# Moving the elementwise work of one streaming-encoder layer from GpSimd to VectorE

## The chip, the core and the metric

The kernel runs on one core of a Trainium2 chip, as one launch. The metric is device microseconds of that core; the median of the three runs of the kernel before is 1533.99 us. PE is TensorE's matrix unit, PEld its weight loads, DVE is VectorE, ACT ScalarE, POOL GpSimd, SP the queue that issues most loads.

## What is computed

One layer over 1024 tokens of width 1024, all in float32. The three branches read one normalised input; their gated sum goes through an output projection, and a SwiGLU feed-forward part follows.

```python
n = rmsnorm(h, norm_mix_pre)
proj = n @ w_in                          # pool input, q, k, v, memory queries, three gates
y_pool = pool_mixer(p_in, w_pool_mix, pool_scale) @ w_pool_o   # trailing means over 2/4/8/16 tokens
y_sb = stick_breaking_attention(q, k, v) @ w_sb_o              # 8 heads, strictly causal
y_x = memory_cross_attention(xq, rmsnorm(mem, norm_mem), w_mem_kv) @ w_x_o
merged = gates[0] * y_pool + gates[1] * y_sb + gates[2] * y_x
h = h + rmsnorm(merged @ w_out, norm_mix_post)
gu = rmsnorm(h, norm_ffn_pre) @ w_ffn_in
ff = (silu(gu[..., :D_FF]) * gu[..., D_FF:]) @ w_ffn_out
h = h + rmsnorm(ff, norm_ffn_post)
```

## The kernel before

Every float32 product is made of three matmuls in a reduced-precision type: each operand is split into a high part (a rounding copy, made by ScalarE) and a low part (operand minus high part, one subtraction of two tiles). `mm3` (L167 to L171) then adds high times high (L169), high times low (L170) and low times high (L171). The low part is the work this document is about. It is made at three places in the code: `split` (L151, subtraction in L164) loads a weight tile and splits it, `parts` (L249 to L251) splits any tile, and `w_parts` calls `parts` for weights. Both take the engine of the subtraction as an argument; most callers leave it at VectorE, and some name `nc.gpsimd`.

The order of the work:

- **Pass over x** (L217 to L235). For each of 8 slices of 128 channels and 2 halves of 512 tokens, ScalarE makes the high part and a square, VectorE the low part (L225), and GpSimd adds the square to the running sum (L233, 14 additions; the first square is written straight into the sum). `pool_step` multiplies.
- **Norms and first operands** (L259 to L306). The memory's sums of squares are added on GpSimd (L294, L297); `rms_rows` makes the row scales, and `inv_root` (L180) takes the power on GpSimd. The operands "11" and "12" of the later products are split, every second one on GpSimd.
- **Operands for Strassen-like products** (L515 to L545). Products by blocks use seven instead of eight multiplications; this needs the operand sums S1 to S4 and "22". Half of S1, all of S4 and all of "22" have their low parts on GpSimd. Three early gate columns (`early`) run in between, with weight low parts on GpSimd.
- **Projections** (`opening`, `pairs`, L436 to L480). Each pair of column blocks takes seven `product` calls. The low parts of the two opening products are GpSimd's, and for the first five pairs also those of S4, S3 and "22". The value projection (L720 to L775) does the same through `two`.
- **Memory attention and pooling** run as background steps between them (`recall`, `pooled`). Of the four pooling groups, the one with window 16 has its product and its sums on GpSimd (`adder`, L649).
- **Stick-breaking attention** (`sticks`, `values`, L835 to L905). ScalarE makes two sigmoids, GpSimd masks them (L856) and sets a start column (L865, L867), VectorE runs a running product (L868) and a multiplication (L874), TensorE transposes (L887) and multiplies with the values (L899, L902). Gate columns fill the gaps (`fill`); each takes a low part on GpSimd (32 in all).
- **Merge and output projection** (L965 to L1060), with weight low parts on GpSimd. These stay.
- **Feed-forward**: eight `opening` calls (L1081), whose 16 weight low parts are on GpSimd, then 11 double blocks and the last product.

Each engine takes its instructions in one fixed order, which the tile framework's scheduler sets when the program is built (from a model of its own), so an instruction that waits holds back all those behind it on the same engine. Loads go through SP's queue, stores through POOL's.

Of the kernel before, what the change touches and what calls it, by code (L numbers as in the profile page):

```python
# [16 lines left out]
KT = D // P  # L17
# [21 lines left out]
def hybrid_block(  # L39
# [177 lines left out]
    for k in range(KT):  # L217
        for c in range(NC):
            xr = t_d()[:, :C]
            load(xr, x[k, c])  # L220
            if c == 0:
                w_units[k] = split(w_pool[k], 3 * P)
            nc.scalar.activation(xgh[k][c], xr, AF.Copy, scale=gain(G_PRE, k))
            xgl[k][c] = (t_b1 if k < 4 else t_b2)(F32R)
            nc.vector.scalar_tensor_tensor(  # L225
                xgl[k][c], xr, gain(G_PRE, k), xgh[k][c].bitcast(F32), ALU.mult, ALU.subtract
            )
            if k == 0:
                nc.scalar.activation(ssum[c], xr, AF.Square)
            else:  # L230
                sq = t_c()[:, :C]
                nc.scalar.activation(sq, xr, AF.Square)
                nc.gpsimd.tensor_add(ssum[c], ssum[c], sq)  # L233
        if k > 3:
            pool_step(k - 4)  # L235
# [43 lines left out]
    for c in range(NC):  # L279
# [24 lines left out]
    for q in range(HK):  # L304
        u = normed_x(q + HK, 0, t_d()[:, :C])
        A["12"][q] = parts(u, t_act(), t_act(), nc.vector if q % 2 else nc.gpsimd)  # L306
# [129 lines left out]
    def opening(raw, sink):  # L436
        (b11, b12), (b21, b22) = raw
        X, Y = ps_a(), ps_a()
        product(X, w_parts(b11, nc.gpsimd), "11", True)
        p1 = copied(X)  # L440
        product(Y, w_parts(b21, nc.gpsimd), "12", True)
# [4 lines left out]
    def pairs(jobs, raws=None, pool=("S4", "S3", "22")):  # L446
# [3 lines left out]

        def some(u, a):
            return w_parts(u, nc.gpsimd if a in pool else nc.vector)

        opened = [opening(raws[j], jobs[j][1]) for j in range(ahead)]
        for j, (_, sink) in enumerate(jobs):
# [6 lines left out]
            product(Y, some(t, "S1"), "S1", True)  # L462
# [3 lines left out]
            product(X, some(t, "S2"), "S2")  # L466
            s2 = copied(X)
            product(Y, some(b22, "S4"), "S4")
# [4 lines left out]
            product(X, some(b12, "S3"), "S3")  # L473
# [5 lines left out]
            product(X, some(b21, "22"), "22")  # L479
# [42 lines left out]
    for q in range(HK):  # L522
# [3 lines left out]
        A["S1"][q] = parts(sums[q], t_act(), t_act(), nc.vector if q % 2 else nc.gpsimd)  # L526
# [7 lines left out]
    for q in range(HK):  # L534
# [3 lines left out]
        A["S4"][q] = parts(u, t_a(F32R), t_a(F32R), nc.gpsimd)  # L538
# [3 lines left out]
    for q in range(HK):  # L542
        A["22"][q] = parts(a22[q], t_act(), t_act(), nc.gpsimd)
# [107 lines left out]
    def pooled(g, c):  # L651
        def step():
            win = 2 << g
            adder = nc.vector if g < 3 else nc.gpsimd
# [7 lines left out]
            adder.tensor_mul(p_in[:, :C], p_in[:, :C], rbc[c])  # L662
            s = p_in
            step_, width = 1, C + 16
            while step_ < win:
                width -= step_
                nxt = t_c()
                adder.tensor_add(nxt[:, :width], s[:, :width], s[:, step_ : step_ + width])
# [63 lines left out]
    def two(us, lo=nc.gpsimd):  # L732
        return [w_parts(u, lo) for u in us]
# [22 lines left out]
    v_product(Y, two(b11, nc.vector), "S1", True)  # L756
# [3 lines left out]
    v_product(X, two(b11, nc.vector), "S2")  # L760
# [40 lines left out]
    pairs([(lambda m=m: quarters(w_gate, m), to_gate(0, m)) for m in range(0, KT, 2)], pool=())  # L801
# [293 lines left out]
    opened = [opening(j, j < HOLD, nc.gpsimd) for j in range(LEAD)]  # L1095
# [297 lines left out]
```

## Time and profile before

| what | us |
|---|---|
| median of 3 runs (lowest, highest) | 1533.99 (1530.56, 1535.62) |
| the profiled execution | 1532.7 |
| its span | 1531.0 |
| PE, DVE, ACT, POOL busy in the span | 1453.5, 1042.6, 705.2, 530.2 |
| mean granted clock of TensorE | 0.984 |

The profile shows one execution. Busy time is the time in which an engine has an instruction under way, so an instruction that stands still inside its own duration counts as busy. The chain that ended last is followed back from the last instruction, at each step to what released it.

### The profile page before, as it was taken

The page shows a single profiled execution, that of the slowest core. Times are in us where ns is not written, and L with a number is a line of the kernel's source. Part 1 is how long each engine was busy: PE and PEld are TensorE (multiplying, and loading weights), DVE is VectorE, ACT ScalarE, POOL GpSimd, SP SyncE. Part 2 cuts the span into 40 slices and gives each one's busy share as a digit, 9 for nine tenths or more (in the row PEclk, how much of TensorE's full clock was granted, in tenths as well). Part 3 has the DMA queues.
Part 4 walks back from the last instruction along what each step waited for, and adds up shares of the span by engine and source line. Part 5 has one row for each costly group of instructions (what it writes and reads, how often), then busy time and mean ns, then how long its engine had stood idle before and what let it go on. Part 6 is the DMA issues. An engine that isn't in the chain of part 4 may idle for free.

```text
span 1531.0 us, 21083 instructions
## 1 busy us (share of the span) xinstructions
PE 1453.5 (95%) x6914; PEld 1201.0 (78%) x6914; DVE 1042.6 (68%) x1593; ACT 705.2 (46%) x1405; POOL 530.2 (35%) x754
## 2 busy tenths in 40 slices
PE   9958999898899999999999999999999999999996
PEld 7747789776788777878888787888888887788875
DVE  8896487896578978756523468675566666578475
ACT  7543465654456656532234665223333333444452
POOL 6674443356434746354456440000011111000011
PEclk9978999999999999999999999999999999999998
DMA  6724553656532523375545554543356555654344
GB/s 218 228 91 134 155 152 120 201 176 201 173 123 86 162 83 118 96 241 190 155 146 184 159 178 160 158 131 124 124 193 197 193 194 193 234 189 146 107 151 158
DMA packets 126222, 245.77 MB, mean 161 GB/s; under 512 B 16656, under 2 KB 20256, under 8 KB 126112
## 3 DMA queue, kind: packets, MB, share of 16 engines
q1 hardware_dynamic: 97952, 173.09, 36.9%
q0 software_dynamic: 27584, 70.29, 13.0%
q8 instruction: 54, 0.88, 0.3%
q10 hardware_dynamic: 576, 1.05, 0.2%
q14 instruction: 56, 0.46, 0.1%
HBM read 174.11 MB, written 69.73 MB: 159 GB/s over the span
## 4 chain that ended last, share of the span: by engine, by line
PE 74%; DVE 10%; issue 5%; DMA 4%; POOL 3%; ACT 3%; SPq 1%; POOLq 0%; DVEq 0%; ACTq 0%
PE pa L169 14%; PE pa L171 14%; PE pa L170 14%; PE pz L171 5%; PE pz L169 5%; PE pz L170 5%; PE pt L169 3%; PE pt L171 3%; PE pt L170 3%; DVE r L868 2%; DMA ws<-in_w_gate_dram 1%; PE pt L887 1%; POOL wl L251 1%; PE pv L169 1%; PE pv L170 1%
## 5 line engine op out<-in xcount | busy, mean ns | idle before, releaser
L169 PE MATMUL pa<-act,wh 128*128 128x512 f32 (+1 forms) x572 | 227.1, 397 | 24.7 <-ACT g L512 10.3
L170 PE MATMUL pa<-act,wh 128*128 128x512 f32 (+1 forms) x572 | 225.2, 394 | 0.0
L171 PE MATMUL pa<-act,wl 128*128 128x512 f32 (+1 forms) x572 | 223.0, 394 | 2.2 <-POOL wl L164 2.2
L250 ACT CAST wh<-b 128x512 fp32r<-128x512 f32 x159 | 98.2, 621 | 164.2 <-PE pa L170 104.1
L169 PEld LDWEIGHTS pa<-act,wh 128*128 128x128 f32 x572 | 109.2, 191 | 49.2 <-ACT g L512 10.7
L163 ACT CAST wh<-ws 128x512 fp32r<-128x512 f32 (+1 forms) x121 | 74.0, 612 | 119.9 <-PE pa L170 33.6
L164 POOL TENSOR_TENSOR wl<-ws,wh 128x512 fp32r<-128x512 f32 x74 | 98.2, 1331 | 88.1 <-ACT wh L163 86.4
L171 PEld LDWEIGHTS pa<-act,wl 128*128 128x128 f32 x572 | 109.2, 191 | 24.8 <-POOL wl L164 2.9
L170 PEld LDWEIGHTS pa<-act,wh 128*128 128x128 f32 x572 | 109.3, 191 | 21.0
L1125 POOL DMA_DIRECT2D ff<-c x44 | 23.7, 540 | 220.4 <-DVE c L1180 130.0
L250 ACT CAST wh<-ws 128x512 fp32r<-128x512 f32 x76 | 47.5, 627 | 110.9 <-DVE ws L1159 43.6
L251 DVE TENSOR_TENSOR wl<-b,wh 128x512 fp32r<-128x512 f32 x116 | 84.3, 727 | 19.0 <-ACT wh L250 14.6
L180 POOL TENSOR_TENSOR rc<-rv,mhalf 128x1 f32<-128x1 f32 (+2 forms) x15 | 14.4, 959 | 203.7 <-DVE rv L1287 199.8
L250 ACT CAST d<-b 128x512 fp32r<-128x512 f32 x66 | 40.8, 621 | 93.1 <-PE pt L170 46.1
L251 DVE TENSOR_TENSOR d<-b,d 128x512 fp32r<-128x512 f32 x66 | 45.3, 689 | 53.1 <-ACT d L250 52.9
L169 PE MATMUL pa<-a,wh 128*128 128x512 f32 x200 | 79.3, 398 | 1.8 <-DVE c L1168 0.8
L170 PE MATMUL pa<-b,wh 128*128 128x512 f32 x196 | 77.4, 395 | 1.5 <-DVE b L225 1.5
L171 PE MATMUL pa<-a,wl 128*128 128x512 f32 x200 | 77.9, 391 | 0.5 <-DVE wl L164 0.5
L868 DVE TENSOR_TENSOR_SCAN r<-a,zero 128x512 f32<-128x512 f32 (+1 forms) x64 | 57.2, 898 | 25.7 <-POOL a L856 25.5
L251 POOL TENSOR_TENSOR wl<-b,wh 128x512 fp32r<-128x512 f32 x43 | 58.8, 1372 | 44.6 <-ACT wh L250 36.6
L175 DVE TENSOR_TENSOR d<-pt,d 128x512 fp32r<-128x512 f32 (+1 forms) x96 | 60.1, 635 | 12.0 <-ACT d L174 11.3
L874 DVE TENSOR_TENSOR b<-b,r 128x512 f32<-128x512 f32 (+2 forms) x96 | 61.3, 643 | 6.7 <-POOL b L856 0.5
(427 smaller groups left out, 4207.0 us busy)
## 6 DMA issues: line engine op xcount, KB each, us to landing
b<-in_w_ffn_in_dram SPq DMA_DIRECT2D x88, 256.0 KB, 2.7
d<-gt SPq DMA_DIRECT2D x48, 256.0 KB, 2.9
ws<-in_w_ffn_in_dram SPq DMA_DIRECT2D x44, 256.0 KB, 2.7
ff<-c POOLq DMA_DIRECT2D x44, 256.0 KB, 3.0
b<-ffS SPq DMA_DIRECT2D x44, 256.0 KB, 2.6
ws<-in_w_gate_dram SPq DMA_DIRECT2D x38, 256.0 KB, 3.7
gt<-g POOLq DMA_DIRECT2D x36, 256.0 KB, 2.5
b<-ff SPq DMA_DIRECT2D x33, 256.0 KB, 3.5
```

Of the source, the lines that this page charges most:

```text
L163: nc.scalar.copy(wh[:, :n], ws[:, :n])
L164: lo.tensor_sub(wl[:, :n], ws[:, :n], wh[:, :n].bitcast(F32))
L169: nc.tensor.matmul(ps, lh, rh, start=first, stop=False, skip_group_check=onto)
L170: nc.tensor.matmul(ps, lh, rl, start=False, stop=False, skip_group_check=onto)
L171: nc.tensor.matmul(ps, ll, rh, start=False, stop=last, skip_group_check=onto)
L175: nc.vector.tensor_sub(lo, ps, hi.bitcast(F32))
L250: nc.scalar.copy(hi, src)
L251: eng.tensor_sub(lo, src, hi.bitcast(F32))
L868: nc.vector.tensor_tensor_scan(ex[:, lo + 1 : C + 1], rest[:, lo:], zero.broadcast_to([P, C - lo]), start, ALU.mult, ALU.add,)
L874: nc.vector.tensor_mul(sg[:, lo:], sg[:, lo:], carry[i][:, lo:C])
L887: nc.tensor.transpose(ptr[:, col + n * P : col + (n + 1) * P], att[i, j // 4][:, (j % 4) * P : (j % 4 + 1) * P], ident,)
L1125: nc.gpsimd.dma_start(ff_d[n][k], t)
```

## The change

The engine argument `nc.gpsimd` is dropped at every `parts`, `w_parts` and `split` up to the end of the attention and in the feed-forward openings, so those low parts go to VectorE; the additions of squares and the pooling of the fourth group go there too. The memory's squares are first added as whole tiles and their halves once at the end (four instructions in place of seven). Masks, start columns, powers and stores stay on GpSimd, as do the low parts of the merge and output projection. By the built programs, 142 instructions leave GpSimd (759 to 617) and 139 come to VectorE (1595 to 1734); line numbers behind the changed places fall by up to six.

```diff
@@ pass over x
-                nc.gpsimd.tensor_add(ssum[c], ssum[c], sq)
+                nc.vector.tensor_add(ssum[c], ssum[c], sq)
@@ operands "11" (and "12", "S1" alike)
-                A["11"][q] = parts(a11[q], t_act(), t_act(), nc.vector if q % 2 else nc.gpsimd)
+                A["11"][q] = parts(a11[q], t_act(), t_act())
@@ squares of the memory
         if q == 0:
-            nc.gpsimd.tensor_add(msum[:, :MEM], sq[:, :MEM], sq[:, MEM:])
+            msq = sq
         else:
-            for i in range(2):
-                nc.gpsimd.tensor_add(
-                    msum[:, :MEM], msum[:, :MEM], sq[:, i * MEM : (i + 1) * MEM]
-                )
+            nc.vector.tensor_add(msq, msq, sq)
+    nc.vector.tensor_add(msum[:, :MEM], msq[:, :MEM], msq[:, MEM:])
@@ opening and pairs (the value projection's `two` alike)
-        product(X, w_parts(b11, nc.gpsimd), "11", True)
+        product(X, w_parts(b11), "11", True)
...
-    def pairs(jobs, raws=None, pool=("S4", "S3", "22")):
+    def pairs(jobs, raws=None):
...
-            return w_parts(u, nc.gpsimd if a in pool else nc.vector)
...
@@ early gate columns
-            gate_step(KT + m, half, 0, split(w_gate[KT + m, half], lo=nc.gpsimd))
+            gate_step(KT + m, half, 0, split(w_gate[KT + m, half]))
@@ operands
-        A["S4"][q] = parts(u, t_a(F32R), t_a(F32R), nc.gpsimd)
+        A["S4"][q] = parts(u, t_a(F32R), t_a(F32R))
...
-        A["22"][q] = parts(a22[q], t_act(), t_act(), nc.gpsimd)
+        A["22"][q] = parts(a22[q], t_act(), t_act())
@@ pooled
-            adder = nc.vector if g < 3 else nc.gpsimd
...
-            adder.tensor_mul(p_in[:, :C], p_in[:, :C], rbc[c])
+            nc.vector.tensor_mul(p_in[:, :C], p_in[:, :C], rbc[c])
@@ fill, in the attention
-                gate_w[t, half] = w_parts(gate_w[t, half], nc.gpsimd)
+                gate_w[t, half] = w_parts(gate_w[t, half])
@@ feed-forward
-    opened = [opening(j, j < HOLD, nc.gpsimd) for j in range(LEAD)]
+    opened = [opening(j, j < HOLD) for j in range(LEAD)]
```

The first place at which the order of the instructions matters is VectorE's queue in the pass over x (`wl` is a weight's low part, `b2` a low part of x, `r_160` and `r_161` the sums of squares). Before:

```order
L164 TENSOR_TENSOR wl_257<-ws_254,wh_256 128x384
L225 SCALAR_TENSOR_TENSOR b2_269<-d_266,g_sb_99,a_153 128x512
L225 SCALAR_TENSOR_TENSOR b2_301<-d_292,g_sb_99,a_154 128x512
L164 TENSOR_TENSOR wl_297<-ws_294,wh_296 128x384
L225 SCALAR_TENSOR_TENSOR b2_309<-d_306,g_sb_99,a_155 128x512
```

Of the change:

```order
L164 TENSOR_TENSOR wl_257<-ws_254,wh_256 128x384
L225 SCALAR_TENSOR_TENSOR b2_269<-d_266,g_sb_99,a_153 128x512
L233 TENSOR_TENSOR r_161<-r_161,c_271 128x512
L225 SCALAR_TENSOR_TENSOR b2_301<-d_292,g_sb_99,a_154 128x512
L233 TENSOR_TENSOR r_160<-r_160,c_303 128x512
L164 TENSOR_TENSOR wl_297<-ws_294,wh_296 128x384
```

One slice of x is now five instructions on VectorE where it was three.

The second place is VectorE's queue where the operands S1, S2 and S4 are made, around 85 us (`act` and `a` are operand parts, `wl_1069` and `wl_1098` weights of the early gate columns; L532, L536 and L537 of before are L527, L531 and L532 of the change). Before:

```order
L532 TENSOR_TENSOR d_1009<-d_1009,c_500 128x512
L532 TENSOR_TENSOR d_998<-d_998,c_493 128x512
L251 TENSOR_TENSOR act_1039<-r_1031,act_1038 128x512
L536 TENSOR_TENSOR c_1158<-act_622,d_998 128x512
L536 TENSOR_TENSOR c_1165<-act_629,d_1009 128x512
L532 TENSOR_TENSOR d_1020<-d_1020,c_507 128x512
```

Of the change:

```order
L164 TENSOR_TENSOR wl_1069<-ws_1066,wh_1068 128x512
L251 TENSOR_TENSOR act_1025<-d_1017,act_1024 128x512
L527 TENSOR_TENSOR d_1006<-d_1006,c_500 128x512
L251 TENSOR_TENSOR act_1036<-r_1028,act_1035 128x512
L531 TENSOR_TENSOR c_1155<-act_619,d_995 128x512
L251 TENSOR_TENSOR act_1204<-d_998,act_1203 128x512
L251 TENSOR_TENSOR a_1137<-d_995,a_1136 128x512
L251 TENSOR_TENSOR act_1208<-d_1009,act_1207 128x512
L527 TENSOR_TENSOR d_1017<-d_1017,c_507 128x512
L251 TENSOR_TENSOR act_1212<-d_1020,act_1211 128x512
L531 TENSOR_TENSOR c_1162<-act_626,d_1006 128x512
L164 TENSOR_TENSOR wl_1098<-ws_1095,wh_1097 128x512
```

The low parts of S1's second half, of "22" (`act_1204` to `act_1212`) and of the gate weights now stand between the sums.

The third place is the attention, POOL's queue first. Before:

```order
L867 COPY r_6701<-r_6679 128x1
L251 TENSOR_TENSOR wl_7091<-ws_6780,wh_7090 128x512
L865 MEMSET r_6744 128x1
L251 TENSOR_TENSOR wl_7271<-ws_6919,wh_7270 128x512
L865 MEMSET r_6747 128x1
L251 TENSOR_TENSOR wl_7362<-ws_6955,wh_7361 128x512
L856 AFFINE_SELECT a_6726<-a_6726 128x128
L856 AFFINE_SELECT b2_6725<-b2_6725 128x128
```

The same stretch of the change, now on VectorE (L862 is the running product, L868 its multiplication, L175 the low part of a transposed tile):

```order
L251 TENSOR_TENSOR wl_7552<-ws_7362,wh_7551 128x512
L862 SCALAR_TENSOR_TENSOR r_6741<-a_6723,zero_110 128x512
L868 TENSOR_TENSOR b2_6722<-b2_6722,r_6741 128x512
L862 SCALAR_TENSOR_TENSOR r_6744<-a_6734,zero_110 128x384
L369 TENSOR_TENSOR b1_5937<-pv_6543,t_6569 64x256
L175 TENSOR_TENSOR d_6709<-pt_6704,d_6708 128x384
```

The three low parts that stood in front of a mask on POOL are gone from there, and a low part now stands in front of a running product on VectorE.

## Rows read from the trace of the kernel before

**Rows 1.** The page, busy us, share of the span and instructions of each engine.
```profile
PE 1453.5 (95%) x6914; PEld 1201.0 (78%) x6914; DVE 1042.6 (68%) x1593; ACT 705.2 (46%) x1405; POOL 530.2 (35%) x754
```

**Rows 2.** Stretches: us, busy us (instructions) by engine, granted clock, DMA share, GB/s.
```profile
0.00:50.00 50.00, 44.48 (x196) 35.74 (x197) 43.01 (x53) 35.82 (x66) 35.55 (x50) 1.00 0.71 231
75.00:120.00 45.00, 26.16 (x93) 19.57 (x92) 44.97 (x43) 18.87 (x36) 30.47 (x21) 0.77 0.27 94
...
400.00:655.00 255.00, 243.23 (x1361) 205.02 (x1362) 209.05 (x297) 156.00 (x350) 124.80 (x267) 1.00 0.35 111
...
840.00:915.00 75.00, 72.08 (x344) 58.49 (x343) 43.31 (x63) 48.12 (x99) 37.51 (x42) 1.00 0.51 162
...
950.00:1000.00 50.00, 50.00 (x223) 41.39 (x222) 33.73 (x54) 14.35 (x25) 3.78 (x7) 1.00 0.48 151
```

**Rows 3.** Chain that ended last, 60 to 125 us: start, us, what.
```profile
by line: DVE c L536 16.4%; DVE a L251 12.5%; DMA c<-c 9.3%; PE pa L169 7.6%; PE pa L170 7.0%; issue 6.8%; PE pa L171 6.7%; DVE c L537 5.4%; DVE b L251 4.3%; DVE d L540 3.8%; DVE d L532 2.8%; DVE d L256 2.6%; DVE r L256 2.0%; DVE d L525 2.0%
...
117.03 0.60 ACT g L512
```

**Rows 4.** Waits of PE, 0 to 150 us: total, times, longest us.
```profile
PE pa L169 <- ACT g L512: 10.3, 1, 10.3
```

**Rows 5.** Timeline of DVE, 94 to 112 us: start, us, instruction.
```profile
95.05 1.75 DVE L251 TENSOR_TENSOR a<-d,a 128x512 fp32r<-128x512 f32 x1
96.73 1.79 DVE L536 TENSOR_TENSOR c<-act,d 128x512 f32<-128x512 f32 x1
...
109.99 0.68 DVE L540 TENSOR_TENSOR d<-d 128x512 f32<-128x512 f32 x1
110.59 0.68 DVE L537 TENSOR_TENSOR c<-act,c 128x512 f32<-128x512 f32 x1
```

**Rows 6.** Timeline of POOL, near 71 us and near 97 us.
```profile
71.05 1.30 POOL L164 TENSOR_TENSOR wl<-ws,wh 128x512 fp32r<-128x512 f32 x1
...
96.22 1.75 POOL L251 TENSOR_TENSOR act<-r,act 128x512 fp32r<-128x512 f32 x1
97.93 1.75 POOL L164 TENSOR_TENSOR wl<-ws,wh 128x512 fp32r<-128x512 f32 x1
```

**Rows 7.** Timeline of DVE in the pass over x.
```profile
4.63 0.56 DVE L164 TENSOR_TENSOR wl<-ws,wh 128x384 fp32r<-128x384 f32 x1 [3.55 <-ACT wh L163]
5.47 0.75 DVE L225 SCALAR_TENSOR_TENSOR b<-d,g_sb,a 128x512 fp32r<-128x512 f32 x1 [0.28 <-ACT a L223]
...
13.65 1.65 DVE L164 TENSOR_TENSOR wl<-ws,wh 128x384 fp32r<-128x384 f32 x1
...
18.63 1.65 DVE L164 TENSOR_TENSOR wl<-ws,wh 128x384 fp32r<-128x384 f32 x1
```

**Rows 8.** Timeline of ACT in the pass over x.
```profile
11.06 0.50 ACT L163 CAST wh<-ws 128x384 fp32r<-128x384 f32 x1
...
13.74 0.50 ACT L163 CAST wh<-ws 128x384 fp32r<-128x384 f32 x1
```

**Rows 9.** Chain that ended last, 330 to 350 us.
```profile
348.82 2.25 DVE c L661
```

**Rows 10.** The page, chain that ended last by line, shares of the span.
```profile
PE pa L169 14%; PE pa L171 14%; PE pa L170 14%; PE pz L171 5%; PE pz L169 5%; PE pz L170 5%; PE pt L169 3%; PE pt L171 3%; PE pt L170 3%; DVE r L868 2%; DMA ws<-in_w_gate_dram 1%; PE pt L887 1%; POOL wl L251 1%; PE pv L169 1%; PE pv L170 1%
```

**Rows 11.** Groups of POOL, 400 to 655 us: busy us, mean ns, idle before.
```profile
L251 POOL TENSOR_TENSOR wl<-ws,wh 128x512 fp32r<-128x512 f32 x25 | 40.2, 1610 | 11.4 <-ACT wh L250 8.1 <-DMA ws<-in_w_gate_dram 3.2
L856 POOL TENSOR_SCALAR_AFFINE_SELECT a<-a 128x128 f32<-128x128 f32 x62 | 31.8, 512 | 25.1 <-ACT a L852 24.7
```

**Rows 12.** Groups of DVE, 400 to 655 us.
```profile
L868 DVE TENSOR_TENSOR_SCAN r<-a,r,zero 128x512 f32<-128x512 f32 x32 | 44.9, 1406 | 17.5 <-ACT a L852 17.4
L874 DVE TENSOR_TENSOR b<-b,r 128x512 f32<-128x512 f32 x47 | 39.5, 842 | 3.1 <-ACT b L853 0.2
```

**Rows 13.** Timeline of DVE, one scan with no wide POOL instruction beside it.
```profile
501.69 1.21 DVE L868 TENSOR_TENSOR_SCAN r<-a,zero 128x512 f32<-128x512 f32 x1
```

**Rows 14.** Waits of ACT, 400 to 655 us.
```profile
ACT wh L250 <- DMA ws<-in_w_gate_dram: 12.3, 5, 8.0
```

More of the change, by code (lines that the diff above doesn't have):

```diff
@@ L305, in hybrid_block @@
         u = normed_x(q + HK, 0, t_d()[:, :C])
-        A["12"][q] = parts(u, t_act(), t_act(), nc.vector if q % 2 else nc.gpsimd)
+        A["12"][q] = parts(u, t_act(), t_act())
     raw_d = [
@@ L438, in opening @@
         X, Y = ps_a(), ps_a()
-        product(X, w_parts(b11, nc.gpsimd), "11", True)
+        product(X, w_parts(b11), "11", True)
         p1 = copied(X)
-        product(Y, w_parts(b21, nc.gpsimd), "12", True)
+        product(Y, w_parts(b21), "12", True)
         nc.vector.tensor_add(p1, Y, p1)
@@ L444, in opening @@
         return X
-    def pairs(jobs, raws=None, pool=("S4", "S3", "22")):
+    def pairs(jobs, raws=None):
         raws = raws or [jobs[0][0]()]
         ahead = len(raws)
-        def some(u, a):
-            return w_parts(u, nc.gpsimd if a in pool else nc.vector)
         opened = [opening(raws[j], jobs[j][1]) for j in range(ahead)]
@@ L461, in pairs @@
             nc.vector.tensor_sub(t, b12, t)
-            product(Y, some(t, "S1"), "S1", True)
+            product(Y, w_parts(t), "S1", True)
             s5 = copied(Y)
@@ L465, in pairs @@
             nc.vector.tensor_sub(t, b22, t)
-            product(X, some(t, "S2"), "S2")
+            product(X, w_parts(t), "S2")
             s2 = copied(X)
-            product(Y, some(b22, "S4"), "S4")
+            product(Y, w_parts(b22), "S4")
             nc.vector.tensor_add(s2, Y, s2)
@@ L472, in pairs @@
             nc.vector.tensor_sub(b12, b22, b12)
-            product(X, some(b12, "S3"), "S3")
+            product(X, w_parts(b12), "S3")
             nc.vector.tensor_add(s5, X, s5)
@@ L478, in pairs @@
                 opened.append(opening(raws[j + 1], jobs[j + 1][1]))
-            product(X, some(b21, "22"), "22")
+            product(X, w_parts(b21), "22")
             sink(1, 0, X)
@@ L525, in hybrid_block @@
         nc.vector.tensor_add(sums[q], sums[q], a22[q])
-        A["S1"][q] = parts(sums[q], t_act(), t_act(), nc.vector if q % 2 else nc.gpsimd)
+        A["S1"][q] = parts(sums[q], t_act(), t_act())
     xq_raws = [quarters(w_xq, 0)]
@@ L667, in step @@
                 nxt = t_c()
-                adder.tensor_add(nxt[:, :width], s[:, :width], s[:, step_ : step_ + width])
+                nc.vector.tensor_add(nxt[:, :width], s[:, :width], s[:, step_ : step_ + width])
                 s = nxt
@@ L730, in v_product, with two @@
                 )
-    def two(us, lo=nc.gpsimd):
-        return [w_parts(u, lo) for u in us]
+    def two(us):
+        return [w_parts(u) for u in us]
     def to_values(c, i, ts):
@@ L755, in hybrid_block @@
     sub2(b11, b12, b11)
-    v_product(Y, two(b11, nc.vector), "S1", True)
+    v_product(Y, two(b11), "S1", True)
     s5 = [copied(t) for t in Y]
@@ L759, in hybrid_block @@
     sub2(b11, b22, b11)
-    v_product(X, two(b11, nc.vector), "S2")
+    v_product(X, two(b11), "S2")
     s2 = [copied(t) for t in X]
@@ L800, in hybrid_block @@
     background += [pooled(g, c) for g in range(4) for c in (1, 0)] + [lambda: fetch(0, 0)]
-    pairs([(lambda m=m: quarters(w_gate, m), to_gate(0, m)) for m in range(0, KT, 2)], pool=())
+    pairs([(lambda m=m: quarters(w_gate, m), to_gate(0, m)) for m in range(0, KT, 2)])
     for q in range(HK):
```

## The prediction

> **What bounds the kernel now.** I read the busy times first, then the stretches, then in the stretches that lose time the chain of work and the single instructions. The page shows PE busy for 95% of the span, DVE for 68%, POOL for 35% [rows 1]. The busy share of PE hides what it loses, because a matmul's duration is longer than the distance to the next one, so I count matmuls. In the feed-forward part PE starts 223 wide matmuls in 50 us, 0.224 us each [rows 2]: nothing can be gained there but by taking matmuls away, and the change takes none. From 75 to 120 us it starts 93, which is 20.8 us of work in 45, at a mean clock of 0.77; in the attention, 400 to 655 us, some of the matmuls are narrow and no count is fair, but PE is busy 243.2 of 255 us while POOL shows 124.8 and DVE 209.0 [rows 2]. The change must earn its time in the first 120 us and in the attention.
>
> From 75 to 120 us DVE is busy 44.97 of 45 us with only 43 instructions [rows 2], and the chain there consists of DVE's operand sums (L536, L537, L540) and low parts (L251); it ends with the sigmoid of L512 at 117.03 [rows 3], for which PE had waited 10.3 us [rows 4]. Why 43 instructions fill 45 us is seen in the timelines. At 109.99 and 110.59 two sums take 0.68 us each and start 0.60 apart; at 95.05 and 96.73 the same kind takes 1.75 and 1.79 [rows 5]. POOL's low part takes 1.30 us at 71.05, but 1.75 at 96.22 and 97.93, where it starts 1.71 after the one before [rows 6]. Where both have work, DVE and POOL take turns: one pair costs 1.70 us on both, nearly the 0.60 and 1.30 of the two alone. DVE's busy time here is mostly standing still.
>
> In the pass over x it is the same: a weight's low part takes 0.56 us at 4.63 and 1.65 at 13.65, and one slice takes 4.98 us (13.65 to 18.63) for three instructions [rows 7].
>
> **The change part by part.** *Pass over x.* GpSimd's 14 additions go, DVE gets 14. A slice on DVE is then two low parts of x (0.75), two additions (0.68) and a weight's low part (0.56) [rows 5, 7], 3.4 us by their durations and about 3.05 by their distances. ScalarE needs 2.68 us per slice (11.06 to 13.74) [rows 8]. TensorE needs 18 matmuls of 0.224, 4.03 us, and so becomes the limit: 0.95 us less on each of the four slices that now take 4.98. **-4 us**; the bounds are 0, if the loads of x set the pace, and -8, if TensorE also recovers what it lost around the row scales. The memory's squares (on DVE three additions at 0.60 and a half-wide one, about 2.2 us, for seven on POOL) lie beside matmuls on the fourth pooling group and the memory's weights that need no row scale, 48 wide and 96 half-wide ones, some 21 us at 0.224; so they cost nothing, and their 2.2 without that cover.
>
> *75 to 120 us.* Here 18 instructions move: two low parts of S1, four gate weights, four of S4, four of "22" and four of the opening products. Alone, 43 and 18 instructions at 0.60 are 36.6 us; three low parts of S3 fall behind the first subtraction for S1 in the new order, so some 35 us stand where 45 stood: -10. PE's gap before 117 us shrinks by as much. Part of the clock comes back as well: 93 matmuls needed 26.2 busy us for 20.8 of work [rows 2], so up to 5 us went to the lower of the two clock levels, which followed on PE's standing still; I take 2. **-12 us**, bounds -5 (the loads of x, or ScalarE, are the next to be late) and -16. By the Trainium skill (SBUF — State Buffer, "SBUF: two separate sides") a VectorE instruction with two SBUF inputs and a GpSimd instruction exclude each other for their whole length; by that rule alone a pair would cost 0.60 and 1.30, and 18 moved instructions would save 18 times 0.70, 12.6 us, where the measured 1.70 gives 18 times 0.50, 9. The trace has the turns but not quite the full sum, so the term stays with the rows.
>
> *120 to 400 us.* 46 weight low parts and the fourth pooling group move, DVE being less full. On the chain stands one contended step, L661 with 2.25 us at 348.82 [rows 9], and a few low parts of POOL that are counted below. **-2 us**, bounds 0 and -4. The stores that POOL issues (q, k, v, xq) are no longer behind low parts; a load waits for few of them, and I count nothing.
>
> *Attention.* On the whole chain POOL's weight low parts hold 1% of the span, 15 us [rows 10], most of it from 120 us to 655. On DVE such an instruction takes 0.68 in place of 1.61 on average [rows 11], which would give back 8 us, if it found DVE free. DVE is busy 209.0 of 255 us [rows 2] and gets 25 of them, 17 us. Against that stand the turns that end: scans take 1.41 us in the mean against 1.21 for one beside which POOL has no wide instruction, over 32 of them 6.3 us; the multiplications 0.84 against 0.68, 47 of them 7.5 us [rows 5, 12, 13]; but masks on POOL go on (31.8 us for one of the two kinds against 40.2 for the low parts [rows 11]), so less than half of these 14 us comes back. DVE thus ends some 11 us fuller, near 220 of 255. What gains most is the order on POOL: masks and start columns no longer stand behind low parts, and the running product waits for them. Each new wait is on DVE: a low part waits for ScalarE's high part, and behind it stand running products, multiplications and the low parts of transposed tiles, for which ScalarE's sigmoids and PE's transposes wait in turn. I take **-7 us** for both, bounds +10 (the added 17 us mostly on the path) and -18 (the 15, and some of the turns).
>
> *Feed-forward openings.* 16 low parts move where DVE is busy 43.3 of 75 us [rows 2]; 11 us more still fit, and PE is fed. **0**; if DVE's norm work were late by then, each would cost 0.68.
>
> The sum is -4, -12, -2 and -7, **-25 us** on the profiled execution's 1532.7, which lies 1.3 under the median of the runs: **1507.7, say 1507**.
>
> **The rivals.**
> 1. *More than that* (0.19): the attention gives its -18 and the first 120 us their bounds in part (-4 and -4 more): about 1490. For it: POOL's masks there show a mean of 0.51 us and both engines contend all along [rows 11, 12]. Against: DVE is fuller there than anywhere in the middle.
> 2. *Another limit stands right behind* (0.13): in the pass over x the loads set the pace (0), from 75 us ScalarE's fixed order does (-5), and the attention gives -3: 1525. For it: ScalarE already needs 2.68 us per slice [rows 8], and the end of the wait at 117 is its sigmoid, queued behind high parts [rows 3].
> 3. *VectorE's queue stands in the attention* (0.07), the slower side. ScalarE's high part of a gate weight waited five times for the load, 12.3 us in all, at most 8.0 [rows 14]. In POOL's queue that held masks; in DVE's queue a low part in wait holds everything. The price is those 12.3 and 25 times a high part and a low part (0.62 and 0.68), 45 us, against 46 us in which DVE is idle [rows 2]. All of it on the path would make 1532.7 - 18 + 45, 1560; it decides for slower as soon as over 18 of the 45 lie on the path. Against: ScalarE, which makes the sigmoids, was held by the same loads before.
> 4. *Busy is busy* (0.03): DVE's 44.97 of 45 us were real work. Then 18 instructions add 12 us there, and 14 in the pass over x, where DVE has 43.0 of 50 us [rows 2], add 9.5, of which 7 find room: about 1548. The Trainium skill (Perfetto Trace Analysis, "Optimizing Scalar/DVE Operations") speaks for it: a saturated VectorE may be relieved by handing work even to GpSimd; the same section warns that the two share a read port. That the same sum takes 0.68 us or 1.79 a few us apart [rows 5] speaks against it.
>
> That the change does not do what it says is excluded by the new order: 142 instructions are gone from POOL and 139 are on DVE.
>
> **How the numbers follow.** The forecast has 0.58, its own range 1495 to 1520. A measurement of this kernel can tell some 0.3%, 4.6 us, from no change. Faster by more: forecast, rival 1 and most of rival 2, 0.87. Within it: the rest of rival 2 and a little of 3, 0.04. Slower: 0.09. The range 1487 to 1528 takes in the forecast, rival 2 and most of rival 1, and leaves out rivals 3 and 4 and the far end of 1, less than 0.2.
>
> **What would show it.** In the new trace the slices of the pass over x should be about 4 us apart and not 5; VectorE's sums around 85 us should all take about 0.68; PE's wait of 10.3 us should be near 0 and the clock from 75 to 120 us above 0.9; scans in the attention should come down towards 1.3, and DVE be busy there about 86%. The prediction is wrong if those durations stay where they are, if PE's matmuls per 50 us in the first 120 us don't rise, or if in the attention DVE's waits for ScalarE's high parts (L250) pass 20 us.

## The result and the profile after

The changed kernel takes **1508.3 us** (median of 4 runs, 1507.4 to 1511.7) against 1533.3 for the kernel before in the same comparison (4 runs, 1530.6 to 1535.6): a ratio of 0.984, 95% interval 0.982 to 0.986, or 25 us less. The profiled execution took 1507.4 us with a span of 1505.7.

The page of the changed kernel, busy us, share of the span and instructions by engine:

```profile
PE 1449.7 (96%) x6914; PEld 1203.1 (80%) x6914; DVE 1037.0 (69%) x1732; ACT 706.1 (47%) x1405; POOL 330.6 (22%) x612
```

Against [rows 1] DVE has 139 instructions more and is busy 5.6 us *less*. What it was busy with before was in part its own standing still.

The stretches of the changed kernel, columns as in [rows 2]:

```profile
0.00:50.00 50.00, 48.29 (x222) 40.32 (x223) 39.85 (x78) 41.05 (x75) 8.20 (x32) 1.00 0.78 256
75.00:120.00 45.00, 38.82 (x153) 30.64 (x154) 41.32 (x69) 25.49 (x45) 4.29 (x8) 0.92 0.36 115
400.00:655.00 255.00, 241.83 (x1331) 204.57 (x1330) 196.24 (x308) 147.05 (x331) 92.77 (x236) 0.98 0.40 127
840.00:915.00 75.00, 72.86 (x328) 58.25 (x327) 62.75 (x104) 49.61 (x98) 13.91 (x26) 1.00 0.54 173
```

In the first 50 us TensorE starts 222 matmuls, not 196; from 75 to 120 us 153, not 93, at a clock of 0.92, not 0.77; DVE does 69 instructions in less busy time than 43 took. The later stretches hold other work than in [rows 2], since everything comes 20 us earlier. The attention therefore has to be compared over the same work: 380 to 632 us here, 403 to 654 us before.

DVE's timeline in the pass over x, changed kernel (start, us, instruction):

```profile
15.39 0.54 DVE L164 TENSOR_TENSOR wl<-ws,wh 128x384 fp32r<-128x384 f32 x1
15.86 0.74 DVE L225 SCALAR_TENSOR_TENSOR b<-d,g_sb,a 128x512 fp32r<-128x512 f32 x1
16.52 0.68 DVE L233 TENSOR_TENSOR r<-r,c 128x512 f32<-128x512 f32 x1
17.12 0.74 DVE L225 SCALAR_TENSOR_TENSOR b<-d,g_sb,a 128x512 fp32r<-128x512 f32 x1
17.78 0.68 DVE L233 TENSOR_TENSOR r<-r,c 128x512 f32<-128x512 f32 x1
18.39 0.55 DVE L164 TENSOR_TENSOR wl<-ws,wh 128x384 fp32r<-128x384 f32 x1
...
85.47 0.68 DVE L532 TENSOR_TENSOR c<-act,c 128x512 f32<-128x512 f32 x1
...
94.50 0.68 DVE L456 TENSOR_TENSOR b<-b,b 128x512 f32<-128x512 f32 x1
```

Five instructions for a slice take 3.00 us (15.39 to 18.39), where three took 4.98 [rows 7]. The last two lines are from the stretch behind: the sums take 0.68 throughout, where [rows 5] had 1.75 and 1.79.

TensorE's waits from 60 to 130 us, changed kernel (total, times, longest):

```profile
PE pa L169 <- ACT wh L163: 4.6, 1, 4.6
PE pa L169 <- DVE c L440: 2.9, 1, 2.9
PE pa L169 <- ACT wh L250: 1.7, 1, 1.7
```

The wait of 10.3 us for the sigmoid [rows 4] is gone. The longest is now for ScalarE's copy of a gate weight, and the chain says why:

```profile
68.09 7.54 DMA ws<-in_w_gate_dram
```

DVE's groups from 400 to 655 us (busy us, mean ns, idle before), changed kernel:

```profile
L862 DVE TENSOR_TENSOR_SCAN r<-a,r,zero 128x512 f32<-128x512 f32 x27 | 34.3, 1278 | 8.1 <-ACT a L846 7.9
L868 DVE TENSOR_TENSOR b<-b,r 128x512 f32<-128x512 f32 x41 | 28.5, 696 | 2.2
L251 DVE TENSOR_TENSOR wl<-ws,wh 128x512 fp32r<-128x512 f32 x21 | 14.3, 686 | 0.8 <-ACT wh L250 0.8
```

The scans fell from 1406 to 1278 ns and the multiplications from 842 to 696 [rows 12]; the low parts that came cost 686 each and waited 0.8 us for ScalarE. Over the same work DVE has 27 instructions more and the same busy time, here (380 to 632 us) and in the kernel before (403 to 654 us: 206.60 us, 295 instructions):

```profile
380.00:632.00 252.00, 241.98 (x1358) 205.76 (x1356) 207.34 (x322) 153.85 (x347) 87.51 (x242) 0.99 0.34 110
```

**Where the 25 us come from.** The table counts TensorE's work: the matmuls of each trace in order of start, 0.2247 us for 512 columns. A lead is how much earlier than in the kernel before TensorE reaches that many us of work. Kernels that are alike up to 100 us of work stand there at 17.8 to 21.0, so single leads are good to some 3 us; the step from one column to the next repeats better.

```
work us        50    100    200    250    350    400    450    550    700   1350
before at      66    144    252    313    428    484    548    672    825   1504
changed       6.9   20.9   22.4   17.3   25.6   23.9   24.0   22.7   22.0   25.0
front_only    6.8   16.7   14.8   15.0   17.0   17.3   17.0   16.4   16.4   15.3
xpass_only    6.1    3.7    3.8    4.1    5.8    6.2    6.2    5.6    6.0    7.6
fill_only    -2.5   -2.9   -1.7   -1.7    2.5    2.9   -0.7    3.2    3.5    2.8
no_fill       7.0   21.0   21.8   16.9   22.9   23.0   20.8   24.2   22.8   24.9
value_gp      6.5   17.8   19.7   18.1   22.0   22.5   20.0   20.6   20.4   23.5
dead_add      1.5   15.7   16.7   11.0   19.5   17.9   17.8   18.2   16.0   19.0
dead_set      5.9   17.6   19.1   14.0   22.1   20.6   19.3   20.8   19.8   22.7
dead_ops      6.3   12.7   13.8    9.4   16.4   14.3   14.4   15.0   10.9   13.4
fill_free     6.4   20.8   21.9   16.6   25.3   26.2   24.2   29.9   29.4   32.9
mix_early     6.7   19.1   20.0   20.1   27.1   28.0   24.7   29.0   27.3   28.8
best          5.9   20.4   22.6   24.2   29.8   30.6   27.5   29.8   28.6   31.3
fill_alt      6.9   20.6   21.9   16.7   19.2   17.4   16.7   21.0   21.2   24.1
```

So 22.4 of the 25 us are there after 200 us of work, 5.1 are lost again right behind, 8.3 come back before and at the head of the attention, and the rest of the attention brings nothing. Of the 8.3, 3.4 come between 280 and 290 us of work (344 to 359 us of the kernel before), where the fourth pooling group stood on GpSimd; `xpass_only`, `front_only` and `fill_only`, which leave it there, gain nothing at that place. Another 4.2 come between 320 and 340 us of work, where even `xpass_only` gains 1.8, though it changes nothing there. No run moves one of these parts alone, except the filler's low parts below. The experiments look into the first 120 us, the loss, and the attention.

### The profile page after: what moved, and what is told of

Read it like the earlier page. It is cut to its first block, busy times and chain, and to the rows that moved or that the text cites. A ratio compares the mean times of both kernels' runs of the same rounds, so it can differ in the third digit from the quotient of the medians.

```text
span 1505.7 us, 20998 instructions
## 1 busy us (share of the span) xinstructions
PE 1449.7 (96%) x6914; PEld 1203.1 (80%) x6914; DVE 1037.0 (69%) x1732; ACT 706.1 (47%) x1405; POOL 330.6 (22%) x612
## 4 chain that ended last, share of the span: by engine, by line
PE 77%; DVE 7%; DMA 6%; issue 5%; ACT 2%; POOL 2%; SPq 1%; POOLq 0%; ACTq 0%; DVEq 0%
PE pa L169 16%; PE pa L170 15%; PE pa L171 15%; PE pz L171 5%; PE pz L170 5%; PE pz L169 5%; PE pt L171 3%; PE pt L169 3%; PE pt L170 3%; DMA ws<-in_w_gate_dram 2%; PE pt L881 1%; SPq L115 1%; DMA d<-in_x_dram 1%; PE pv L893 1%; PE pv L896 1%
## 5 line engine op out<-in xcount | busy, mean ns | idle before, releaser
L251 DVE TENSOR_TENSOR wl<-b,wh 128x512 fp32r<-128x512 f32 x159 | 108.1, 685 | 36.4 <-ACT wh L250 23.6
L164 POOL TENSOR_TENSOR wl<-ws,wh 128x512 fp32r<-128x512 f32 x52 | 67.8, 1311 | 78.0 <-ACT wh L163 78.0
L164 DVE TENSOR_TENSOR wl<-ws,wh 128x512 fp32r<-128x512 f32 (+1 forms) x69 | 46.1, 672 | 52.1 <-ACT wh L163 32.6
L175 DVE TENSOR_TENSOR d<-pt,d 128x512 fp32r<-128x512 f32 (+1 forms) x96 | 60.8, 637 | 16.7 <-ACT d L174 16.2
L174 ACT CAST d<-pt 128x512 fp32r<-128x512 f32 (+1 forms) x96 | 52.7, 557 | 29.3 <-PE pt L881 15.1
L862 DVE TENSOR_TENSOR_SCAN r<-a,zero 128x512 f32<-128x512 f32 (+1 forms) x64 | 53.4, 842 | 15.4 <-POOL a L850 14.6
```

The lines of the kernel that those rows point to most:

```text
L164: lo.tensor_sub(wl[:, :n], ws[:, :n], wh[:, :n].bitcast(F32))
L174: nc.scalar.copy(hi, ps)
L175: nc.vector.tensor_sub(lo, ps, hi.bitcast(F32))
L251: eng.tensor_sub(lo, src, hi.bitcast(F32))
L862: nc.vector.tensor_tensor_scan(ex[:, lo + 1 : C + 1], rest[:, lo:], zero.broadcast_to([P, C - lo]), start, ALU.mult, ALU.add,)
```

## The experiments

The theory of the prediction is contention: GpSimd's instructions that read SBUF lengthen VectorE's two-input instructions beside them, and that lengthening was the loss. Its rival is latency: GpSimd's results came late, and somebody waited for them. For the attention the question is another one, whether VectorE's busy time lies on the path there or not. Runs of the kernel before spread from 1530 to 1543 us over the chips used, those of one changed kernel by 1 to 6; variants are compared by their medians with ranges and by the table.

**One part alone: the first 120 us.** On the kernel before, the additions of the squares, the memory's squares, and the low parts of "11", "12", S1, S4, "22" and the early gates go to VectorE; the opening products stay:

```diff
-                nc.gpsimd.tensor_add(ssum[c], ssum[c], sq)
+                nc.vector.tensor_add(ssum[c], ssum[c], sq)
...
-            gate_step(KT + m, half, 0, split(w_gate[KT + m, half], lo=nc.gpsimd))
+            gate_step(KT + m, half, 0, split(w_gate[KT + m, half]))
...
-        A["S4"][q] = parts(u, t_a(F32R), t_a(F32R), nc.gpsimd)
+        A["S4"][q] = parts(u, t_a(F32R), t_a(F32R))
```

> The kernel before, with only the work up to the operands moved to VectorE: the 14 additions of squares, the memory's squares, and the low parts of 11, 12, S1, S4, 22 and of the six early gate weights. Theory 1 (VectorE and GpSimd take turns in the first 120 us, and that is nearly all the change is worth): 19 to 22 us less than before, about 1512. Theory 2 (the terms of the prediction): 16 less there, about 1517, the rest lies in the attention. If the gain lies behind 120 us: within 5 us of before.

Measured: 1517.6 us (1514.6 to 1518.7), ratio 0.987, interval 0.985 to 0.989. That is 19 us under the median of the kernel before in the same comparison (1536.2), but 15.2 by the spans of the profiled executions (1531.0 and 1515.8), so it does not decide between the two figures expected, 16 and 19 to 22; it is 15 to 20 us of the 25. Its lead is 16.7 at 100 us of work and 15.3 at the end: behind the first 120 us it gains nothing more. What the changed kernel has more there (20.9 - 16.7 at 100, 22.4 - 14.8 at 200) goes with the low parts of the opening products and the pairs, which were left out here.

**The 14 additions alone.** Only the first pair of lines above:

> The kernel before, with the 14 additions of the squares in the pass over x moved to VectorE and nothing else. T1: the slices of the pass come 4 us apart and not 5, the time is 4 to 7 us less than that of the kernel before; the first weight low parts after the pass stay late, so that most of the 21 us of lead at 144 us is still missing. T2 (the loads of x set the pace): 0 to -1.

Measured: 1526.8 us (1525.0 to 1529.2), ratio 0.993, interval 0.992 to 0.995, which is 7 to 13 us, at or above what was expected; by the spans of the profiled executions (1531.0 and 1523.7) it is 7.3, and the lead is 6.1 at 50 us of work and 7.6 at the end. TensorE's waits in it, 60 to 130 us, and its stretch 75 to 120 us:

```profile
PE pa L169 <- ACT g L512: 9.0, 2, 5.7
PE pa L169 <- DVE r L525: 5.4, 1, 5.4
PE pa L171 <- POOL wl L164: 4.2, 1, 4.2
```

```profile
75.00:120.00 45.00, 29.70 (x89) 22.59 (x90) 43.08 (x39) 19.69 (x36) 31.10 (x22) 0.70 0.15 53
```

The waits of the stretch behind stay, as does its pace: 89 matmuls at a clock of 0.70. The two parts are separate gains.

**Is it the contention? Dead work on GpSimd.** To the changed kernel, work is added on GpSimd whose results nobody uses. First, 14 additions of a tile to itself in the pass over x:

```diff
                 nc.vector.tensor_add(ssum[c], ssum[c], sq)
+                nc.gpsimd.tensor_add(dead, dead, dead)
```

> GpSimd gets 14 additions of an unrelated 128x512 tile to itself in the pass over x, and nobody waits for them. T1 (VectorE's instructions are lengthened by GpSimd's instructions that run beside them): although no result of GpSimd is used, the slices of the pass go back from 4 us towards 5, VectorE's additions and low parts beside them take 1.6 to 1.8 us and not 0.6 to 0.7, and the kernel is 4 to 7 us slower than the changed one: 1512 to 1515. T2 (what the change took away was a wait for GpSimd's slow result): 0, 1508, the durations stay.

VectorE's timeline in it, and the row of GpSimd's timeline beside it:

```profile
14.80 1.52 DVE L235 TENSOR_TENSOR r<-r,c 128x512 f32<-128x512 f32 x1
...
19.14 1.39 DVE L166 TENSOR_TENSOR wl<-ws,wh 128x384 fp32r<-128x384 f32 x1
20.46 1.52 DVE L227 SCALAR_TENSOR_TENSOR b<-d,g_sb,a 128x512 fp32r<-128x512 f32 x1
21.90 1.52 DVE L235 TENSOR_TENSOR r<-r,c 128x512 f32<-128x512 f32 x1
23.35 0.74 DVE L227 SCALAR_TENSOR_TENSOR b<-d,g_sb,a 128x512 fp32r<-128x512 f32 x1
24.01 0.68 DVE L235 TENSOR_TENSOR r<-r,c 128x512 f32<-128x512 f32 x1
...
11.65 11.23 POOL L236 TENSOR_TENSOR g<-g 128x512 f32<-128x512 f32 x8
```

GpSimd's eight additions end at 22.88 us; from the next instruction on VectorE's durations are 0.74 and 0.68 again. The time: 1513.6 us (1512.5 to 1517.3), 5 us more than the changed kernel and than the next run, which was made on the same chip, and the lead at 50 us of work falls to 1.5. No result was waited for, so latency cannot have it.

Second, 42 memsets in the same place, three with each of VectorE's additions, which write and read nothing:

```diff
                 nc.vector.tensor_add(ssum[c], ssum[c], sq)
+                for _ in range(3):
+                    nc.gpsimd.memset(dead, 0.0)
```

> GpSimd gets 42 memsets of an unrelated 128x512 tile in the same pass over x, three per chunk, which write SBUF and read nothing; nobody waits for them. T1a (GpSimd's reading is what VectorE runs up against): VectorE's durations there stay at 0.6 to 0.7 us, time 1508. T1b (any GpSimd instruction of that width is): VectorE's additions take over 1.2 us and the kernel is 4 to 15 us slower. T2: 0, like T1a.

Its VectorE and GpSimd rows:

```profile
12.31 0.68 DVE L235 TENSOR_TENSOR r<-r,c 128x512 f32<-128x512 f32 x1
12.91 0.55 DVE L166 TENSOR_TENSOR wl<-ws,wh 128x384 fp32r<-128x384 f32 x1
...
11.75 14.58 POOL L237 MEMSET g<- 128x512 f32 x25
```

GpSimd is busy without a gap, and VectorE's durations stay: 1508.8 us (1508.1 to 1510.2). Writing alone lengthens nothing here. The Trainium skill (SBUF — State Buffer, "SBUF: two separate sides") says the same: VectorE's two-input instructions are locked out only by a GpSimd instruction that reads SBUF.

Third, a copy and 30 additions of half that width from about 70 us on:

```diff
         A["S1"][q] = parts(sums[q], t_act(), t_act())
+        if q == 0:
+            dead = small.tile([P, MEM], F32, tag="t", name="t", bufs=2)
+            nc.gpsimd.tensor_copy(dead, A["S1"][0][0][:, :MEM].bitcast(F32))
+            for _ in range(30):
+                nc.gpsimd.tensor_add(dead, dead, dead)
```

> GpSimd gets one copy and 30 additions of an unrelated 128x256 tile from about 75 us on, which nobody waits for but GpSimd's own stores behind them. T1 (contention): VectorE's instructions between 75 and 110 us take 1.1 us and more in place of 0.60 to 0.68, the subtractions for S1 come 8 to 15 us later, PE's clock falls as in the kernel before, and the kernel is 8 to 18 us slower than the changed one: 1516 to 1526. T2 (late results of GpSimd were the cause): 0, within 2 us of 1508.

VectorE's timeline in it:

```profile
92.33 1.10 DVE L537 TENSOR_TENSOR c<-act,c 128x512 f32<-128x512 f32 x1
93.35 1.09 DVE L251 TENSOR_TENSOR a<-d,a 128x512 fp32r<-128x512 f32 x1
94.37 0.68 DVE L164 TENSOR_TENSOR wl<-ws,wh 128x512 fp32r<-128x512 f32 x1
94.97 0.68 DVE L251 TENSOR_TENSOR wl<-b,wh 128x512 fp32r<-128x512 f32 x1
```

Measured: 1520.2 us (1519.3 to 1523.1), 12 us more, with the clock at 0.85 from 75 to 120 us. GpSimd's stores of gate tiles stand behind some of these additions, so a part of the 12 may be theirs; of the 12, 8.2 us are there at 100 us of work (20.9 against 12.7).

**The attention: the filler's low parts.** Three kernels vary only the subtraction in `fill`:

```diff
-                gate_w[t, half] = w_parts(gate_w[t, half])
+                gate_w[t, half] = w_parts(gate_w[t, half], nc.gpsimd)
```

This is `no_fill`, on the changed kernel; `fill_only` is the opposite, the kernel before with the engine dropped at this one place; `fill_alt` gives GpSimd every second one (`nc.gpsimd if half else nc.vector`).

> The changed kernel, with only the 32 low parts of the gate weights in the attention put back on GpSimd. Theory 1: within 3 us of the changed kernel's 1508. Theory 2: 7 us more than it, 1515. If the added work on VectorE costs something in the attention that the first 120 us hide: 3 to 8 us less, about 1503.

> The kernel before, with only the 32 low parts of the gate weights in the attention moved to VectorE. Theory 1 (the attention is held by its chain of sigmoid, mask, running product, transposes and products, not by GpSimd's queue): within 3 us of before. Theory 2 (the prediction): 7 us less. Rival 3 of the prediction (a waiting low part holds VectorE's queue): 10 us more or worse.

> The changed kernel with every second low part of the gate weights in the attention on GpSimd again. Both ends (all on VectorE, 1508; all on GpSimd, 1510) measured alike, and without these low parts it is 9 us less. If a low part costs what it takes of either engine's share, the half lies between the ends, within 2 us of 1509; if VectorE's fullness alone costs (and contention nothing), 3 to 5 us less than the changed kernel.

Measured: `no_fill` 1510.4 us (1507.7 to 1512.9), `fill_alt` 1508.9 (1508.4 to 1509.2), the changed kernel 1508.3 (1507.4 to 1511.7). `fill_only` 1530.4 (1527.3 to 1533.7), ratio 0.997, interval 0.995 to 0.998, 5 us less than before. In the table that gain stands between 250 and 350 us of work, at the head of the attention, where `xpass_only` also gains 1.8; inside it nothing is added. So the engine of these low parts is worth 3 to 5 us on the kernel before and at most 2 on top of the rest.

The fourth kernel leaves them out; its third product then uses the high part where the low part belongs, which leaves the low part's share out of 32 gate products:

```diff
-                gate_w[t, half] = w_parts(gate_w[t, half])
+                wh = wpool.tile([P, C], F32R, tag="wh", name="wh", bufs=5)
+                nc.scalar.copy(wh, gate_w[t, half])
+                gate_w[t, half] = wh, wh
```

> The changed kernel without the 32 low parts of the gate weights that fill the attention: the high part is used in place of the low part, so matmuls stay the same in number and the low part's product is left out of the result's accuracy. VectorE then has 32 instructions, 22 us of busy time, less in the attention. T1 (VectorE's busy time there is off the path): within 3 us of the changed kernel, 1505 to 1511. T3 (VectorE's added low parts ate what the end of the contention gave back): 7 to 17 us faster, 1491 to 1501.

Measured: **1499.6 us** (1499.0 to 1502.2), 8.7 less than the changed kernel and 9.2 less than `dead_set` on the same chip, where 7 to 17 stood for a path that runs over VectorE. Its stretch 380 to 632 us:

```profile
380.00:632.00 252.00, 243.57 (x1370) 208.35 (x1368) 194.43 (x298) 152.53 (x345) 87.67 (x241) 0.99 0.35 112
```

and that of `no_fill`:

```profile
380.00:632.00 252.00, 240.94 (x1349) 204.34 (x1349) 206.00 (x293) 151.01 (x342) 120.58 (x267) 1.00 0.35 111
```

VectorE is busy 12.9 us less without them than in the changed kernel's row above, though the stretch then holds some more of the later work. In the table the lead grows by 4.6 between 350 and 550 us of work, where that of the changed kernel falls by 2.9; `no_fill` and `fill_alt`, which keep the low parts, gain 1.3 and 1.8 there, so 3 to 7 us of the step are due to leaving them out. With the low parts on GpSimd VectorE is just as busy (206.0 us) with 29 instructions less than in the changed kernel, so its other instructions take that much longer. Whichever engine makes these low parts, they cost about 9 us. That they cost it as VectorE's busy time is not shown: without them a gate product also no longer waits for a low part. TensorE's waits that end with one are only 1.3 us in the changed kernel (380 to 632 us), but no run keeps the wait and takes only the work away, or the other way round.

**The loss between values and gates.** All kernels that move the values' low parts and leave the order of loads alone lose 4.4 to 5.7 us between 200 and 250 us of work. VectorE's timeline of the changed kernel there:

```profile
246.20 0.42 DVE L586 TENSOR_REDUCE st<-pz 128x1 f32<-128x256 f32 x1 [0.16 <-PE pz L585]
249.03 0.69 DVE L164 TENSOR_TENSOR wl<-ws,wh 128x512 fp32r<-128x512 f32 x1 [2.41 <-ACT wh L163]
249.64 0.68 DVE L175 TENSOR_TENSOR d<-pt,d 128x512 fp32r<-128x512 f32 x1
```

and ScalarE's wait, 235 to 290 us:

```profile
ACT wh L163 <- DMA ws<-in_w_mix_dram: 3.2, 1, 3.2
```

The mixing weight is loaded when the values end. ScalarE stands 3.2 us for the load, VectorE 2.41 us for ScalarE, and then VectorE has no gap:

```profile
250.00:255.00 5.00, 4.14 (x24) 3.41 (x22) 5.00 (x13) 4.24 (x13) 2.22 (x5) 1.00 0.99 348
255.00:260.00 5.00, 2.97 (x13) 2.08 (x13) 5.00 (x16) 3.04 (x9) 0.67 (x2) 0.72 0.61 192
```

It is full for ten us, and TensorE, with 13 matmuls in the second five, waits for it; its granted clock falls to 0.72 there. In the kernel before, the same low part stood on VectorE and waited 0.17 us:

```profile
269.92 0.69 DVE L164 TENSOR_TENSOR wl<-ws,wh 128x512 fp32r<-128x512 f32 x1 [0.17 <-ACT wh L163]
```

The 15 us behind it held three low parts of weights on VectorE, where the changed kernel has five. One kernel gives the values' low parts back to GpSimd, but for S1 and S2:

```diff
-    def two(us):
-        return [w_parts(u) for u in us]
+    def two(us, lo=nc.gpsimd):
+        return [w_parts(u, lo) for u in us]
```

> The changed kernel, with the 10 low parts of the value projection that had been on GpSimd put back there. Between 250 and 296 us the changed kernel loses about 5 us of the 22 it is ahead. If VectorE, fuller by these low parts, causes it: 4 to 6 us less, about 1503. If it is the order of the instructions or the lower clock there, and not these low parts: within 2 us of 1508.

Measured: 1507.3 us (1506.1 to 1509.1); the loss at this place is 1.6 and not 5.1, but less comes back after it. ScalarE waits only 0.8 us for the mixing weight here, so this kernel does not have the stand either. The other keeps the change and issues the load at the start of the value part:

```diff
     (b11, b12), (b21, b22) = raw
+    mix_ws = wpool.tile([P, C], F32, tag="ws", name="ws", bufs=3)
+    load(mix_ws, w_mix)
...
-    mix_h, mix_l = split(w_mix)
+    mix_h = wpool.tile([P, C], F32R, tag="wh", name="wh", bufs=5)
+    mix_l = wpool.tile([P, C], F32R, tag="wl", name="wl", bufs=5)
+    with tc.high_priority():
+        nc.scalar.copy(mix_h, mix_ws)
+        nc.vector.tensor_sub(mix_l, mix_ws, mix_h.bitcast(F32))
```

> The changed kernel with the load of the mixing weight issued at the start of the value part instead of at its end, so that its low part on VectorE no longer stands 2.4 us in front of the queue, waiting for ScalarE's high part and that for the load. If this stand is what lost 5 us of the lead between the values and the gates, the time is 2 to 5 us less than that of the changed kernel, 1503 to 1506; if the loss comes of VectorE being full there (17 low parts that GpSimd made before), 0 to -1.

Measured: 1505.2 us (1503.5 to 1506.0). The step from 200 to 250 us of work is now +0.1. TensorE's waits from 235 to 290 us:

```profile
PE pz L584 <- ACT c L590: 1.8, 1, 1.8
PE pz L584 <- DVE st L586: 0.7, 2, 0.4
PE pa L169 <- DVE d L355: 0.4, 1, 0.4
```

The early load takes the loss away, but not by taking the stand away. VectorE now stands as long for the high part of the next weight, whose load is late in its turn, and is full for the ten us from 255 on:

```profile
251.32 0.69 DVE L251 TENSOR_TENSOR wl<-b,wh 128x512 fp32r<-128x512 f32 x1 [2.56 <-ACT wh L250]
```

So a stand of 2.5 us in front of a full queue does not by itself cost 5 us here. What else the late load of the mixing weight held up is open.

Both together:

> The changed kernel with GpSimd keeping the low parts of the value weights (all but S1 and S2) and the mixing weight's load issued at the start of the value part. The first alone gave 1507, and a loss of 2 in place of 5 us between the values and the gates. If the two losses there add, 1502 to 1506, a version that beats both; if something else is late next, 1506 to 1509.

Measured: **1503.4 us** (1500.4 to 1506.6), ratio to the kernel before 0.978, interval 0.976 to 0.980. The step is +1.6. Its four runs lie below the four of the changed kernel, which ran in another comparison; against `fill_alt`, which measures like the changed kernel and ran on the same chip, it is 5.5 us less. So a version that beats both is the change with an earlier load and with the values' low parts left where they were. That the second part adds anything is not clear: `mix_early` alone, on the same chip, has 1503.5 to 1506.0, inside the range of both together.

## Why the prediction was right, and where its terms were not

The total of -25 us came out, the terms less so: they are off by 3 to 6 us each, and that the errors cancel to nothing is luck. By the table:

| term | predicted | measured |
|---|---|---|
| pass over x | -4 | -6.9 (50 us of work) |
| 75 to 120 us, with what follows to 200 us of work | -12 | -15.5 (22.4 - 6.9) |
| 120 to 400 us | -2 | +1.1 (lead 22.4 to 21.3 at 325 us of work, 396 us before) |
| attention | -7 | -0.7 (21.3 to 22.0) |
| feed-forward openings and the rest | 0 | -3.0 (22.0 to 25.0) |

**The pass over x.** Mechanism right, term too small, inside its bounds (0 to -8). I gave TensorE back 0.95 us on four slices. In fact it starts 182 matmuls of 512 columns in the first 50 us where it started 152, and those 30 are 6.7 us at 0.2247. From 8 to 28 us it starts 88 of them, one each 0.227 us, where it started 74, and its waits in the first 60 us are nearly gone:

```profile
PE pt L145 <- DVE zero L139: 1.1, 1, 1.1
PE pa L169 <- ACT a L223: 0.6, 1, 0.6
```

TensorE is the limit, as said. VectorE does a slice in 3.00 us, close to the 3.05 it was priced at, so its slices are not 4 us apart as I wrote they would be, because it runs ahead of TensorE.

**75 to 120 us.** Right in kind: the durations are 0.60 apart, the sigmoid's wait is gone, the clock is 0.92. The subtraction for S1 (L456, L461 before) starts at 94.50, where it started at 115.74:

```profile
115.74 0.68 DVE L461 TENSOR_TENSOR b<-b,b 128x512 f32<-128x512 f32 x1
```

The term stays under its bound of -16. What stands behind it is partly rival 2: TensorE's next longest wait (4.6 us) is for a gate weight, whose load took 7.54 us.

**120 to 400 us.** The step that failed is "On the chain stands one contended step": I looked for what the change takes off the chain and not for what it puts in front of VectorE's queue. It looks like rival 3 in a place I had not searched: a low part on VectorE waits for ScalarE's high part and that for a load, and the change makes the queue behind it longer. That it had waited before too, by 0.17 us, was in the trace. Issuing the load earlier took the loss away (-5.1 became +0.1), leaving the values' low parts on GpSimd most of it (-1.6). That the stand is the cause is not shown, since with the early load VectorE stands 2.56 us for another weight and loses nothing; what the late load does beyond that stays open. The gain that the term did name came, and more: the 3.4 us between 280 and 290 us of work are where L661 and the fourth pooling group stood.

**The attention.** Two steps failed, in opposite directions. "Less than half of these 14 us comes back" was too low: on the 32 scans and 47 multiplications of [rows 12], 128 and 146 ns each, 4.1 and 6.9, 11 of 14 came back. For the scans that is all there was. The 1.21 us of [rows 13] belong to a scan without a start column (`r<-a,zero`); one with it (`r<-a,r,zero`), as in [rows 12], takes 1.28 with nothing beside it, in the kernel before too:

```profile
545.01 1.28 DVE L868 TENSOR_TENSOR_SCAN r<-a,r,zero 128x512 f32<-128x512 f32 x1
```

The masks that stay do not lengthen the scans; it is the masks that wait. One takes 0.29 us alone, and one that starts while a scan has more than 0.1 us to go ends just after the scan: in the changed kernel in all 21 such cases, in 20 of them by 0.08 to 0.09 us:

```profile
497.96 1.23 DVE L862 TENSOR_TENSOR_SCAN r<-a,zero 128x512 f32<-128x512 f32 x1
498.12 1.15 POOL L850 TENSOR_SCALAR_AFFINE_SELECT b<-b 128x128 f32<-128x128 f32 x1 [0.20 <-ACT b L847]
499.23 0.29 POOL L850 TENSOR_SCALAR_AFFINE_SELECT a<-a 128x128 f32<-128x128 f32 x1
```

So the two engines still take turns there, at GpSimd's cost. DVE did not become 11 us fuller but stayed the same (207.3 us to 206.6), 82% of the stretch and not 86. "What gains most is the order on POOL" brought nothing: the running product waited 8.3 us for GpSimd's masks before, and does so 8.0 us now. With VectorE as busy as before the time stayed as before. `fill_free` fits this, but does not show that it is VectorE's time that counts. That moving the filler's low parts brought 3 to 5 us when done alone and next to none on top of the rest means that terms measured apart do not add here; which of VectorE's instructions are on the path was not tried.

**The feed-forward openings.** Taken at nothing; from 700 to 800 us of work TensorE needs 113.2 us here, 112.6 to 113.4 in the other kernels that move these low parts, 114.9 in the kernel before and 116.8 in `front_only`, which leave them. So -2 and not 0: small, but the same in all of them.

**The rivals.** More than that (1) falls with the attention, which gave nothing of its -18. Busy is busy (4) falls with DVE's busy time and with the dead additions. VectorE's queue standing in the attention (3) falls with 0.8 us of waits for high parts, where over 20 would have been needed. Another limit (2) is there, but behind the gain and not in place of it.

## What to carry to other kernels

An engine that the profile shows as full may be standing still inside its instructions: compare the duration of one instruction with the same one a few us away, and ask which other engine is working when it is long. If the other engine reads the same memory, moving its work *onto* the full engine can make that engine less busy; dead work on the other engine, which nobody waits for, is a clean test of it. And before work is put into a queue, look at what already waits in that queue for a load: here a wait of 0.17 us became 2.4 where a lead of 5 was lost, and issuing that load earlier brought 3 to 4 us of the whole time.

## What the runs showed of the hardware

- A GpSimd addition of 128x512 beside VectorE's (1.40 us each, 11.23 us for eight) stretches VectorE's additions from 0.68 to 1.52 us, and its scaled low parts from 0.74 to 1.52; one of 128x256 stretches 0.68 to 1.10. The effect ends with the last of them.
- A GpSimd memset of 128x512 takes 0.58 us (14.58 for 25) and stretches nothing on VectorE.
- GpSimd's masks in the attention (128x128) leave VectorE's scans at 1278 ns (1.28 us with nothing beside) and its multiplications at 696 (0.68 alone), so the contention that I had left to them was nearly all that of the low parts. The masks pay instead: 0.29 us alone, and up to 1.26 when they start during a scan, until just after its end.
